# A PEER layer on one core: one-hot matrices built one token at a time, and a gate table with its rows in another order

## The chip, the cores and the metric

The kernel runs on one core of a Trainium2 chip. The metric is the device time of one execution in microseconds (us). Most executions agree within 0.3%. Five engines work side by side, each through its own instructions in order: PE (TensorE, matrix products into PSUM; PEld is its weight load), DVE (VectorE), ACT (ScalarE), POOL (GpSimd) and SP (SyncE), which here only issues transfers. Sixteen DMA engines carry out the transfers.

## The reference, cut to what matters

A decoder layer with three kinds of attention, an output projection, and a PEER feed-forward layer over 512 tokens. In the PEER part every token has 8 heads, each head picks 16 experts out of 128 x 128 by two sets of sub-keys, and the result of a token is the sum over its 128 chosen experts of gelu(u_e . h) times the gate, times v_e:

```python
expert = jnp.take_along_axis(cand_idx, pos, axis=-1)     # i1 * 128 + i2
gate = jax.nn.softmax(top_s, axis=-1)
...
a = jnp.einsum('cd,ced->ce', x_c, u[e_c])
w = jax.nn.gelu(a.astype(jnp.float32), approximate=False).astype(x_c.dtype) * g_c
return jnp.einsum('ce,ced->cd', w, v[e_c])
```

## The kernel before, in words

The attention, the projections and the query products come first. Then the 512 tokens are split in two. The 128 tokens of chunk `GC` are served by gathers: `gather_all` (lines 479 to 494) fetches one row of `u` or `v` per token and slot with an indirect DMA that POOL issues (line 475) and works on it with DVE (line 482 for `u`, line 493 for half of `v`) or with ACT and POOL (the other half). The other 384 tokens (three chunks, `DC`) are served densely: all 16384 experts are applied to all tokens, in 128 blocks of 128 experts, and a gate table says how much each expert counts for each token, mostly nothing.

Each block takes two products. `a_block` (line 521) multiplies a block of `u` with the 384 tokens, in 24 matmuls of 384 columns, and takes the gelu with ACT (line 527). `w_block` (line 628) multiplies that with the gates (line 645) and the result with a block of `v`, in 18 matmuls of 512 columns, which stay in PSUM as running sums over all 128 blocks. `u_parts` (line 514) prepares a block of `u`: SP loads it into one of three `flat` buffers (line 516), ACT writes the high part (line 86) and POOL the low part (line 87) into one of four places of `yT`.

The gate table is made in the stage that the diff touches (lines 577 to 602). For every token the 128 pairs (i1, i2) and their gates lie on the 128 partitions, as columns of `iT`. One matmul per token turns them into a 128 x 128 table: the one-hot matrix of i1, 128 slots x 128 keys, times the one-hot matrix of i2 with the gate in it. Four tokens form a group: DVE compares four columns of i1 with `iota` in one instruction of 512 elements (line 591), the same for i2 (line 592), and the gate goes in with one DVE instruction of 512 elements in every second group (line 595), and with four ACT instructions in the others (line 597). Then come four matmuls (line 600) and one ACT copy into `stage` (line 601), which holds 32 tokens as 128 keys i1 on the partitions x 128 keys i2 x 32 tokens. There are 96 groups and 12 `stage` tiles in two buffers. Line 602 writes each `stage` to a DRAM tile of its own, `gd[ci_][q]`, with the same order of axes, 16 KB in one run per partition.

In the same stretch of time 64 of the 128 `a_block`s run ahead, and their results go to DRAM (`ad`, line 607); half of the 128 `u` gathers are put beside them. From line 613 on `w_block` runs over the 128 blocks, inline `a_block`s for the other 64 blocks between them. Every four blocks it loads the gates of four blocks (`NB = 4`) from the 12 tiles: 12 transfers (line 637) in runs of 32 tokens, 128 bytes.

Tile, the layer that the kernel is written in, makes the order of instructions on each engine from the order of the source, the dependencies and a model of their times, and puts in the waits. `bank("s")` gives one of four PSUM banks.

Of the kernel before, what the change touches and what calls it, by code (L numbers as in the profile page):

```python
# [11 lines left out]
F32 = mybir.dt.float32  # L12
# [4 lines left out]
AF = mybir.ActivationFunctionType  # L17
ALU = mybir.AluOpType
# [4 lines left out]
P = 128  # L23
# [7 lines left out]
NK = 128  # L31
# [5 lines left out]
DC = [c for c in range(NT) if c != GC]  # L37
NSP = 64
GT = 32
LEAD = 2  # L40
NB = 4
# [3 lines left out]
SCB = 4  # L45
UL = "GGGG"
EM = 4
OGD = "AV"
GR = 1.0
TD = P * len(DC)  # L50
GROUPS = ((0, 1, 2), (3, 4, 5), (6, 7))
# [5 lines left out]
def layer_kernel(ctx, tc, x, xT, memT, mem, w_in, w_kv, w_out, w_q, cols, qk_gain, g_bc, subT, bias_tab,  # L57
                 uT, u, v, out):
    nc = tc.nc
    V, A, G, T, DMA = nc.vector, nc.scalar, nc.gpsimd, nc.tensor, nc.sync  # L60

    def tile_pool(**kw):
        return tc.tile_pool(reuse_waits="tile", **kw)

    top = ctx.enter_context(tc.tile_pool(name="top", bufs=1))
    dram = ctx.enter_context(tc.tile_pool(name="dram", bufs=1, space=DRAM))
    st = ctx.enter_context(tile_pool(name="st", bufs=8))
    xd = [dram.tile([P, D], F32, name=f"xd{c}") for c in range(NT)]
    gd = [[dram.tile([P, NK, GT], F32, name=f"gd{c}_{q}") for q in range(P // GT)] for c in range(len(DC))]
    ad = [dram.tile([P, TD], F32, name=f"ad{b}") for b in range(NSP)]  # L70

    ident = top.tile([P, P], F32, name="ident")
# [3 lines left out]
    iota = top.tile([P, NK], F32, name="iota")  # L76
# [8 lines left out]
    def split(hi, lo, src, e_lo=None):  # L85
        A.activation(hi, src, AF.Copy)  # L86
        return (e_lo or V).tensor_sub(lo, src, hi.bitcast(F32))  # L87
# [27 lines left out]
    def bank(tag=None):  # L115
        if tag is None:
            tag = CYC[turn[0] % len(CYC)]
            turn[0] += 1
        return pps.tile([P, S], F32, tag=tag, name=tag, bufs=BANKS[tag])

    def quarters(t):
        return t.rearrange("p (a b) -> p a b", b=P)
# [356 lines left out]
    def gather_all():  # L479
        for s_ in range(NSLOT):  # L480
            row = gather(u, s_)
            V.scalar_tensor_tensor(row, row, 1.0, hg, ALU.mult, ALU.mult, accum_out=av[:, s_:s_ + 1])  # L482
            yield
        ge = peer.tile([P, NSLOT], F32, name="ge")
        A.activation(ge, av, AF.Gelu)
        V.tensor_mul(gw, ge, gate_g)
        for s_ in range(NSLOT):
            row = gather(v, s_)
            if s_ % 2:
                A.activation(row, row, AF.Copy, scale=gw[:, s_:s_ + 1])  # L490
                G.tensor_add(ga[1], ga[1], row)  # L491
            else:
                V.scalar_tensor_tensor(ga[0], row, gw[:, s_:s_ + 1], ga[0], ALU.mult, ALU.add)  # L493
            yield
# [35 lines left out]
    with tile_pool(name="qa", bufs=1) as qa, tile_pool(name="qp", bufs=2) as qp:  # L530
# [5 lines left out]
        for n in range(4):  # L536
# [5 lines left out]
            w = [w_pieces[n, k2] for k2 in range(KD // 2)]  # L542
# [34 lines left out]
    with tile_pool(name="oh", bufs=2) as oh:  # L577
        loaded = 0
        steps = gather_all()
        for ci_, c in enumerate(DC):  # L580
            iT = oh.tile([P, 3, P], F32, tag="iT", name="iT")
            route(c, iT)
            for q in range(P // GT):
                stage = oh.tile([P, NK, GT], F32, tag="stage", name="stage")
                for t4 in range(0, GT, 4):
                    t0 = q * GT + t4
                    bc = lambda a: a[:, t0:t0 + 4, None].to_broadcast([P, 4, NK])
                    ib = iota[:, None, :].to_broadcast([P, 4, NK])
                    o1 = oh.tile([P, 4, NK], F32, tag="o1", name="o1", bufs=3)
                    o2 = oh.tile([P, 4, NK], F32, tag="o2", name="o2", bufs=3)  # L590
                    V.tensor_tensor(o1, bc(iT[:, 0, :]), ib, ALU.is_equal)  # L591
                    V.tensor_tensor(o2, bc(iT[:, 1, :]), ib, ALU.is_equal)  # L592
                    og = oh.tile([P, 4, NK], F32, tag="og", name="og", bufs=3)
                    if OGD[t4 // 4 % len(OGD)] == "V":
                        V.tensor_mul(og, o2, bc(iT[:, 2, :]))  # L595
                    for j in range(0 if OGD[t4 // 4 % len(OGD)] == "V" else 4):
                        A.activation(og[:, j, :], o2[:, j, :], AF.Copy, scale=iT[:, 2, t0 + j:t0 + j + 1])
                    gp = quarters(bank("s"))
                    for j in range(4):
                        T.matmul(gp[:, j, :], o1[:, j, :], og[:, j, :], start=True, stop=True)  # L600
                    A.activation(stage[:, :, t4:t4 + 4].rearrange("p e t -> p t e"), gp, AF.Copy)
                DMA.dma_start(gd[ci_][q], stage)
        for b in range(NSP):
            while loaded < min(b + 4, NSP):
                u_parts(loaded, loaded % 4, dict(G=G, V=V)[UL[loaded % len(UL)]])
                loaded += 1
            DMA.dma_start(ad[b], a_block(b))
            for s_ in range(int(GR * b), int(GR * (b + 1))):
                with tc.issue_after(last_lo[-1].ins):
                    next(steps)  # L610

    vs_src = v.rearrange("(a b) w -> b a w", b=NK)
    with tile_pool(name="vb", bufs=2) as vb:
        acc = [[bank("ssssoo"[2 * c + n]) for n in range(2)] for c in range(len(DC))]
        inl, spl = (list(range(r0, r1, NB)) for r0, r1 in ((NSP, NK), (0, NSP)))
        starts, a, b = [], 0, 0
        while a + b < len(inl) + len(spl):
            if a < len(inl) and (b == len(spl) or a < LEAD or (a - LEAD) * len(spl) <= b * (len(inl) - LEAD)):
                starts.append(inl[a])
                a += 1  # L620
            else:
                starts.append(spl[b])
                b += 1
        order = [b + i for b in starts for i in range(NB)]
        later = {b: a for b, a in zip([b for b in order if b >= NSP], [b for b in order if b >= NSP][1:])}
        gtiles = {}

        def w_block(n, b, ag):
            if ag is None:
                ag = vb.tile([P, TD], F32, tag="agr", name="agr", bufs=3)  # L630
                DMA.dma_start(ag, ad[b])
            g0 = b // NB * NB
            if g0 not in gtiles:
                gt = vb.tile([P, NB, len(DC), P], F32, tag="gt", name="gt")
                for ci_ in range(len(DC)):
                    for q in range(P // GT):
                        DMA.dma_start(gt[:, :, ci_, q * GT:(q + 1) * GT], gd[ci_][q][:, g0:g0 + NB, :])
                gtiles[g0] = gt
            gt = gtiles[g0]
            vr = vb.tile([P, D], F32, tag="vr", name="vr", bufs=3)  # L640
            DMA.dma_start(vr, vs_src[b])
            vs = [t.rearrange("p k t -> p (k t)")[:, (2 + n % 2) * D:(3 + n % 2) * D] for t in yT]
            split(vs[0], vs[1], vr)
            w = vb.tile([P, TD], F32, tag="w", name="w")
            V.tensor_mul(w.rearrange("p (c t) -> p c t", t=P), ag.rearrange("p (c t) -> p c t", t=P),  # L645
                         gt[:, b % NB, :, :])
            ws = [vb.tile([P, TD], F32R, tag=f"ws{i}", name=f"ws{i}") for i in range(2)]
            split(ws[0], ws[1], w)
            for ci_ in range(len(DC)):
                for k in range(2):  # L650
                    mm3(acc[ci_][k], [t[:, ci_ * P:(ci_ + 1) * P] for t in ws],
                        [t[:, k * 512:(k + 1) * 512] for t in vs], n == 0, n == NK - 1)

        pend = None
        for n, b in enumerate(order):
            if b >= NSP:
                for a in (b, later.get(b)):
                    if a is not None and a not in halves and a >= loaded:
                        u_parts(a, a % 2, G)
                        loaded = a + 1  # L660
                ag = a_block(b)
            else:
                ag = None
            if pend is not None:
                w_block(*pend)
            pend = (n, b, ag)
        w_block(*pend)
        for _ in steps:
            pass
        for c in [GC] + DC:  # L670
            xr = vb.tile([P, D], F32, tag="xr", name="xr", bufs=3)
            DMA.dma_start(xr, xd[c])
            if c == GC:
                for t in ga:
                    V.tensor_add(xr, xr, t)
            else:
                for k in range(2):
                    sl = xr[:, k * 512:(k + 1) * 512]
                    V.tensor_add(sl, sl, acc[DC.index(c)][k])
            DMA.dma_start(out[c * P:(c + 1) * P, :], xr)  # L680
# [59 lines left out]
```

## Time and profile before

| | |
|---|---|
| time, median of 3 runs | 1754.59 us (1750.6 to 1756.23) |
| span of the profiled execution, first to last instruction | 1749.3 us |
| PE busy | 1592.6 us (91%) |
| DVE busy | 1442.9 us (82%) |
| POOL busy | 968.3 us (55%) |
| ACT busy | 787.2 us (45%) |
| DMA | 390.08 MB in 317463 packets, 214944 of them under 512 B |

The profile is one execution. The page gives its span and no other time of its own; the runs, timed without a profile, lie 1.3 to 6.9 us above the span. Busy time is the union of the instructions of an engine; matmuls overlap each other, so a busy PE is not always at its peak, and two DVE instructions in a row overlap by some 0.08 us in the records, so that the cost of one is the time from its start to the next start. An engine that waits for a memory port is shown as busy.

### The profile page before, as it was taken

The numbers are of one execution on the slowest core, as the hardware profiler recorded it, in microseconds if no ns is written. First come the engines' busy times: TensorE is split into PE (matmuls) and PEld (weight loads), VectorE is DVE, ScalarE is ACT, GpSimd is POOL, SyncE is SP. The second block draws the span as 40 slices with busy tenths as digits, with TensorE's granted clock in tenths as the row PEclk, the third lists the DMA queues.
The fourth block names the chain that finished last, engine by engine and source line by source line (L and its number), as shares of the span: only waits on it lengthen the run. The fifth ranks groups of instructions, "written<-read, shape, count | busy, mean of one in ns | idle before, by whom it ended". The sixth has DMA issues, their size and how long they took to land.

```text
span 1749.3 us, 23459 instructions
## 1 busy us (share of the span) xinstructions
PE 1592.6 (91%) x8045; PEld 1397.1 (80%) x8045; DVE 1442.9 (82%) x2552; ACT 787.2 (45%) x1287; POOL 968.3 (55%) x531
## 2 busy tenths in 40 slices
PE   7999989997686878878999999999999999899997
PEld 6886667997686777778998888888888888788885
DVE  6556745899999999979956877877889978889896
ACT  6345633332332555667843333334444443444442
POOL 4220013363776675734465544456778867788774
PEclk9999999998888989889999999999999999999998
DMA  8302034132566566557699999998999999898894
GB/s 322 106 25 103 1 121 144 49 125 90 181 212 198 182 218 216 176 222 280 231 315 325 279 318 288 315 286 279 291 287 278 317 290 275 255 309 276 288 277 171
DMA packets 317463, 390.08 MB, mean 223 GB/s; under 512 B 214944, under 2 KB 240544, under 8 KB 314656
## 3 DMA queue, kind: packets, MB, share of 16 engines
q1 hardware_dynamic: 280480, 254.36, 46.0%
q0 software_dynamic: 36864, 134.23, 21.6%
q8 instruction: 63, 1.03, 0.2%
q14 instruction: 56, 0.46, 0.1%
HBM read 346.57 MB, written 41.94 MB: 222 GB/s over the span
## 4 chain that ended last, share of the span: by engine, by line
PE 49%; DVE 36%; issue 5%; DMA 5%; ACT 2%; SPq 2%; POOL 2%; DVEq 0%; ACTq 0%; POOLq 0%
PE s L96 7%; PE s L97 7%; PE s L95 6%; PE t L95 5%; PE t L97 5%; PE t L96 5%; DVE row L482 5%; DVE o L591 5%; DVE o L592 4%; PE o L96 3%; PE o L97 3%; PE o L95 3%; DVE eq L440 2%; PE o L330 2%; DVE og L595 2%
## 5 line engine op out<-in xcount | busy, mean ns | idle before, releaser
L87 POOL TENSOR_TENSOR yT<-flat,yT 128x1024 fp32r<-128x1024 f32 x128 | 346.6, 2709 | 216.4 <-ACT yT L86 208.7
L95 PE MATMUL t<-hT,yT 128*128 128x384 f32 x1024 | 351.4, 343 | 26.1 <-ACT ag L527 26.1
L97 PE MATMUL t<-hT,yT 128*128 128x384 f32 x1024 | 351.4, 343 | 2.4 <-POOL yT L87 2.4
L96 PE MATMUL t<-hT,yT 128*128 128x384 f32 x1024 | 350.3, 342 | 0.0
L87 DVE TENSOR_TENSOR yT<-vr,yT 128x1024 fp32r<-128x1024 f32 x128 | 209.5, 1637 | 54.7 <-ACT yT L86 51.5
L475 POOL DMA_INDIRECT row<-u,exp_g x128 | 161.7, 1263 | 124.0 <-DVE row L482 88.3
L95 PEld LDWEIGHTS t<-hT,yT 128*128 128x128 f32 x1024 | 197.0, 192 | 32.5 <-ACT ag L527 27.3
L96 PE MATMUL s<-yT,ws 128*128 128x512 f32 x512 | 206.7, 405 | 11.1 <-DVE yT L87 10.8
L482 DVE SCALAR_TENSOR_TENSOR row<-row,hg 128x1024 f32<-128x1024 f32 x128 | 189.2, 1482 | 24.0 <-DMA row<-u,exp_g 24.0
L97 PE MATMUL s<-yT,ws 128*128 128x512 f32 x512 | 201.4, 402 | 4.2 <-DVE ws L87 4.2
L475 POOL DMA_INDIRECT row<-v,exp_g x128 | 156.1, 1219 | 84.9 <-DVE ga L493 49.6
L86 ACT ACTIVATE ws<-w 128x384 fp32r<-128x384 f32 x128 | 67.1, 524 | 299.4 <-DVE w L645 118.7
L97 PEld LDWEIGHTS t<-hT,yT 128*128 128x128 f32 x1024 | 196.8, 192 | 5.7 <-POOL yT L87 3.0
L96 PEld LDWEIGHTS t<-hT,yT 128*128 128x128 f32 x1024 | 196.8, 192 | 4.5
L86 ACT ACTIVATE yT<-flat 128x1024 fp32r<-128x1024 f32 x128 | 135.4, 1058 | 144.2 <-issue 53.6
L491 POOL TENSOR_TENSOR ga<-ga,row 128x1024 f32<-128x1024 f32 x64 | 164.1, 2564 | 26.1 <-ACT row L490 25.4
L95 PE MATMUL s<-yT,ws 128*128 128x512 f32 x512 | 165.1, 399 | 7.8 <-ACT ws L86 7.8
L86 ACT ACTIVATE yT<-vr 128x1024 fp32r<-128x1024 f32 x128 | 134.2, 1048 | 57.4 <-DMA vr<-v 44.0
L600 PE MATMUL s<-og,o 128*128 128x128 f32 x768 | 109.7, 296 | 54.8 <-DVE og L595 38.4
L600 PEld LDWEIGHTS s<-og,o 128*128 128x128 f32 x768 | 103.1, 208 | 63.4 <-issue 39.6
L87 DVE TENSOR_TENSOR ws<-w,ws 128x384 fp32r<-128x384 f32 x128 | 119.8, 937 | 41.0 <-ACT ws L86 36.2
L493 DVE SCALAR_TENSOR_TENSOR ga<-row,gw,ga 128x1024 f32<-128x1024 f32 x64 | 143.2, 2238 | 6.6 <-DMA row<-v,exp_g 6.4
(268 smaller groups left out, 3249.2 us busy)
## 6 DMA issues: line engine op xcount, KB each, us to landing
flat<-uT SPq DMA_DIRECT2D x128, 512.0 KB
vr<-v SPq DMA_DIRECT2D x128, 512.0 KB
gd<-stage SPq DMA_DIRECT2D x12, 2048.0 KB
gt<-gd SPq DMA_DIRECT2D x384, 64.0 KB
ad<-ag SPq DMA_DIRECT2D x64, 192.0 KB
agr<-ad SPq DMA_DIRECT2D x64, 192.0 KB
wraw<-w_in SPq DMA_DIRECT2D x8, 1024.0 KB
flat<-w_q SPq DMA_DIRECT2D x16, 512.0 KB
```

Of the source, the lines that this page charges most:

```text
L86: A.activation(hi, src, AF.Copy)
L87: return (e_lo or V).tensor_sub(lo, src, hi.bitcast(F32))
L95: T.matmul(o, ah, bh, start=start, stop=False)
L96: T.matmul(o, ah, bl, start=False, stop=False)
L97: T.matmul(o, al, bh, start=False, stop=stop)
L475: G.indirect_dma_start(out=row, out_offset=None, in_=table, in_offset=bass.IndirectOffsetOnAxis(ap=exp_g[:, s_:s_ + 1], axis=0))
L482: V.scalar_tensor_tensor(row, row, 1.0, hg, ALU.mult, ALU.mult, accum_out=av[:, s_:s_ + 1])
L491: G.tensor_add(ga[1], ga[1], row)
L493: V.scalar_tensor_tensor(ga[0], row, gw[:, s_:s_ + 1], ga[0], ALU.mult, ALU.add)
L591: V.tensor_tensor(o1, bc(iT[:, 0, :]), ib, ALU.is_equal)
L592: V.tensor_tensor(o2, bc(iT[:, 1, :]), ib, ALU.is_equal)
L600: T.matmul(gp[:, j, :], o1[:, j, :], og[:, j, :], start=True, stop=True)
```

## The change

The comparison with i1 and the one with i2 become one DVE instruction each per token, of 128 elements, with the token's column of `iT` as a scalar operand (one value per partition). The second instruction also multiplies with the gate, a second scalar operand. The tile `og`, its DVE instruction and its four ACT instructions go. The gate table becomes one DRAM tile with the axes block (i2), expert (i1), token; line 602 writes it in runs of 32 tokens, and every four blocks it is read by one transfer in runs of 384 tokens. Line 645 then multiplies tiles that are contiguous.

```diff
-OGD = "AV"
...
-    gd = [[dram.tile([P, NK, GT], F32, name=f"gd{c}_{q}") for q in range(P // GT)] for c in range(len(DC))]
+    gd = dram.tile([NK, P, TD], F32, name="gd")
...
-                    bc = lambda a: a[:, t0:t0 + 4, None].to_broadcast([P, 4, NK])
-                    ib = iota[:, None, :].to_broadcast([P, 4, NK])
                     o1 = oh.tile([P, 4, NK], F32, tag="o1", name="o1", bufs=3)
                     o2 = oh.tile([P, 4, NK], F32, tag="o2", name="o2", bufs=3)
-                    V.tensor_tensor(o1, bc(iT[:, 0, :]), ib, ALU.is_equal)
-                    V.tensor_tensor(o2, bc(iT[:, 1, :]), ib, ALU.is_equal)
-                    og = oh.tile([P, 4, NK], F32, tag="og", name="og", bufs=3)
-                    if OGD[t4 // 4 % len(OGD)] == "V":
-                        V.tensor_mul(og, o2, bc(iT[:, 2, :]))
-                    for j in range(0 if OGD[t4 // 4 % len(OGD)] == "V" else 4):
-                        A.activation(og[:, j, :], o2[:, j, :], AF.Copy, scale=iT[:, 2, t0 + j:t0 + j + 1])
+                    for j in range(4):
+                        i1, i2, gate = (iT[:, i, t0 + j:t0 + j + 1] for i in range(3))
+                        V.tensor_scalar(o1[:, j, :], iota, i1, None, ALU.is_equal)
+                        V.tensor_scalar(o2[:, j, :], iota, i2, gate, ALU.is_equal, ALU.mult)
                     gp = quarters(bank("s"))
                     for j in range(4):
-                        T.matmul(gp[:, j, :], o1[:, j, :], og[:, j, :], start=True, stop=True)
+                        T.matmul(gp[:, j, :], o1[:, j, :], o2[:, j, :], start=True, stop=True)
...
-                DMA.dma_start(gd[ci_][q], stage)
+                DMA.dma_start(gd[:, :, ci_ * P + q * GT:ci_ * P + (q + 1) * GT].rearrange("b p t -> p b t"), stage)
...
-                gt = vb.tile([P, NB, len(DC), P], F32, tag="gt", name="gt")
-                for ci_ in range(len(DC)):
-                    for q in range(P // GT):
-                        DMA.dma_start(gt[:, :, ci_, q * GT:(q + 1) * GT], gd[ci_][q][:, g0:g0 + NB, :])
+                gt = vb.tile([P, NB, TD], F32, tag="gt", name="gt")
+                DMA.dma_start(gt, gd[g0:g0 + NB].rearrange("b p t -> p b t"))
...
-            V.tensor_mul(w.rearrange("p (c t) -> p c t", t=P), ag.rearrange("p (c t) -> p c t", t=P),
-                         gt[:, b % NB, :, :])
+            V.tensor_mul(w, ag, gt[:, b % NB])
```

## Rows read from the trace of the kernel before

**Rows 1.** By stretch: busy us of PE, PEld, DVE, ACT, POOL; clock, DMA share, GB/s.

```profile
560.00:880.00 320.00, 265.24 (x1661) 256.54 (x1660) 311.09 (x375) 204.66 (x367) 181.59 (x82) 0.93 0.60 217
900.00:1700.00 800.00, 781.62 (x3686) 674.21 (x3685) 660.58 (x561) 334.39 (x431) 537.18 (x306) 1.00 0.93 293
```

**Rows 2.** The chain that ended last, 560 to 880 us, shares by line.

```profile
by line: DVE o L591 24.8%; DVE o L592 23.5%; DVE row L482 15.0%; DVE og L595 10.9%; DMA row<-u,exp_g 6.6%; DVE eq L440 4.4%; DVE ex L443 3.9%; issue 3.4%; DVE eq L442 3.1%; PE s L600 1.5%; DVE pe L447 0.7%; PE t L97 0.5%; PE t L96 0.4%; PE 
```

**Rows 3.** Groups by line, 560 to 880: busy us, mean ns | idle before, releasers.

```profile
L591 DVE TENSOR_TENSOR o<-iT,iota 128x512 f32<-128x512 f32 x96 | 96.7, 1022 | 0.0
L592 DVE TENSOR_TENSOR o<-iT,iota 128x512 f32<-128x512 f32 x96 | 89.5, 955 | 0.0
L595 DVE TENSOR_TENSOR og<-o,iT 128x512 f32<-128x512 f32 x48 | 41.6, 868 | 0.0
L87 POOL TENSOR_TENSOR yT<-flat,yT 128x1024 fp32r<-128x1024 f32 x37 | 113.9, 3080 | 127.0 <-ACT yT L86 126.8
L475 POOL DMA_INDIRECT row<-u,exp_g x37 | 48.7, 1317 | 5.6 <-issue 2.6 <-PE s L600 0.2
```

**Rows 4.** Timeline of DVE, then of POOL beside it: start us, duration us.

```profile
562.82 2.88 DVE L592 TENSOR_TENSOR o<-iT,iota 128x512 f32<-128x512 f32 x1
565.62 0.68 DVE L591 TENSOR_TENSOR o<-iT,iota 128x512 f32<-128x512 f32 x1
566.22 0.68 DVE L592 TENSOR_TENSOR o<-iT,iota 128x512 f32<-128x512 f32 x1
...
562.23 2.92 POOL L87 TENSOR_TENSOR yT<-flat,yT 128x1024 fp32r<-128x1024 f32 x1 [3.65 <-ACT yT L86]
565.30 1.24 POOL L475 DMA_INDIRECT row<-u,exp_g  x1
```

**Rows 5.** Timeline of DVE: scalar operand per partition, then a constant.

```profile
145.40 0.28 DVE L313 TENSOR_SCALAR p<-p,den 128x128 f32<-128x128 f32 x1
145.59 0.15 DVE L312 RECIPROCAL den<-den 128x1 f32<-128x1 f32 x1
...
553.72 0.21 DVE L464 TENSOR_SCALAR e<-ei 128x128 int32<-128x128 int32 x1
553.86 0.21 DVE L465 TENSOR_SCALAR e<-ei 128x128 int32<-128x128 int32 x1
```

**Rows 6.** Groups by form: the same operation from PSUM, and a blocked CAST.

```profile
L217 DVE TENSOR_SCALAR vt<-s,rx 128x128 f32<-128x128 f32 x2 | 0.7, 343 | 0.0
L421 DVE CAST tf<-ti 128x128 f32<-128x128 uint32 x3 | 3.4, 1121 | 0.0
```

**Rows 7.** DMA queues, 560 to 880, then 900 to 1700: packets, MB, share.

```profile
q1 hardware_dynamic: 12240, 49.75, 43.1%
...
q1 hardware_dynamic: 236289, 136.84, 58.5%
q0 software_dynamic: 26640, 97.01, 33.9%
gt<-gd SPq DMA_DIRECT2D x377, 64.0 KB
```

**Rows 8.** Timeline of SP's transfers: start us, time to issue them, how many.

```profile
880.58 0.32 SPq L602 DMA_DIRECT2D gd<-stage  x1
882.97 0.32 SPq L607 DMA_DIRECT2D ad<-ag  x1
...
887.56 11.18 SPq L637 DMA_DIRECT2D gt<-gd  x6
...
908.55 6.17 SPq L607 DMA_DIRECT2D ad<-ag  x1
914.77 8.73 SPq L637 DMA_DIRECT2D gt<-gd  x10
...
934.41 12.87 SPq L637 DMA_DIRECT2D gt<-gd  x10
```

**Rows 9.** The chain that ended last, 738 to 780 us: start us, us.

```profile
740.17 10.87 DMA row<-u,exp_g
```

More of the change, by code (lines that the diff above doesn't have):

```diff
@@ L644, in w_block @@
             w = vb.tile([P, TD], F32, tag="w", name="w")
-            V.tensor_mul(w.rearrange("p (c t) -> p c t", t=P), ag.rearrange("p (c t) -> p c t", t=P),
-                         gt[:, b % NB, :, :])
+            V.tensor_mul(w, ag, gt[:, b % NB, :])
             ws = [vb.tile([P, TD], F32R, tag=f"ws{i}", name=f"ws{i}") for i in range(2)]
```

## The prediction

> **What bounds the kernel now.** I read the busy times by stretch first. In the stage that makes the gate table, 560 to 880 us, DVE is busy for 311.1 of 320 us and PE for 265.2; from 900 to 1700 us PE is busy for 781.6 of 800 [rows 1]. So the stage is DVE's and what follows is PE's, with 55 us of idle PE in the one and 18.4 us in the other. The chain that ended last says the same: in the stage the two comparisons and the DVE half of the gate product hold 59% of it, the gather product of line 482 another 15% [rows 2]. A microsecond that DVE loses or wins there should move the end; one in the later stretch counts only as far as it touches PE's 18.4 us.
>
> The groups of the stage show how DVE's time is made up [rows 3]. The 240 instructions of lines 591, 592 and 595 are busy for 227.8 us. In the timeline an undisturbed one starts 0.60 us after the one before and is shown with 0.68 us; another takes 2.88 us, and beside that one POOL works on line 87 from 562.23 to 565.15 [rows 4]. 240 x 0.68 = 163 us, so some 65 us of the 227.8 are time behind POOL.
>
> **The change part by part.** First DVE's own work. Now: 240 x 0.60 = 144 us. After: 384 tokens x 2 = 768 instructions of 128 elements. The nearest row is the softmax scaling, 128x128 with one scalar operand per partition, source and result in SBUF: it starts at 145.40 and the next starts at 145.59, 0.19 to 0.20 us (12 such) [rows 5]. With a constant in its place the step is 0.14 us (553.72 to 553.86), so I put the operand at 0.06 us. Line 591's successor: 384 x 0.195 = 75 us. Line 592's has two such operands, and no row shows that; I take another 0.06 us, 384 x 0.255 = 98 us, since the first cost that much. Together 173 us, +29 us. Bounds: 0.14 us for all, if the operands cost nothing here, gives 104 us, -40 us; the same operation with its source in PSUM lasts 0.343 us [rows 6], some 0.265 from start to start, which gives 204 us, +60 us.
>
> Four small instructions per comparison thus cost DVE about what the one large one did: 8 x 0.195 = 1.56 us a group against 2.5 x 0.60 = 1.50 us, even with the gate free of charge. The 192 ACT instructions that go I cost at nothing: ACT is busy for 204.7 of the 320 us [rows 1], and is no line of the stage's chain [rows 2].
>
> Second, the wait behind POOL. The 37 low parts of line 87 keep their number and their length. A small CAST of 128x128 also waits: its three come to 1.12 us on average [rows 6], though such a one lasts 0.21 us undisturbed. I leave the 65 us as they are. If smaller steps let POOL in less often or more often, that is worth -65 us at most, and upward the rest of POOL's 113.9 us, +49 us.
>
> Third, POOL's indirect DMAs. The comparison at 565.62 lasted its 0.68 us although POOL was issuing a gather from 565.30 to 566.54 [rows 4], so they do not hold a comparison of two tensors. No row shows a scalar-operand instruction beside a gather alone. Bounds: nothing, or all 48.7 us of the 37 gathers [rows 3]; I take 10 us, nearer to the row that shows no wait. The Trainium skill, in "SBUF — State Buffer", section "Who interferes with whom", says that a `tensor_scalar` whose operands allow it runs in a mode that takes the port pair shared with GpSimd whole, and that the generation of descriptors needs that pair's write side, while a two-tensor instruction takes the read side only. The undisturbed comparison agrees with the second half; by the first half the whole of it, 49 us, would come into the sum in place of 10.
>
> Fourth, the writes of the gate table. A `stage` of 2 MB now leaves in 128 runs of 16 KB, after the change in 128 x 128 = 16384 runs of 128 bytes. The table of before is read in such runs, and from 900 to 1700 us one can price them [rows 7]. The gathers' queue q0 moved 97.01 MB in 33.9% of 16 x 800 us, 22.4 bytes per ns. Queue q1 moved 136.84 MB in 58.5%, 7488 us of engine time; 377 x 64 KB = 24.7 MB of it, in 193,000 runs, are the gate loads, and the other 112.1 MB at 22.4 bytes per ns make 5005 us. That leaves 2483 us, an estimated 12.9 ns a run. One write is then 16384 x 12.9 / 16 = 13.2 us on all 16 engines, against 5.9 us for 2.1 MB at 22.4 bytes per ns. In the stage the DMA engines have 0.60 of 320 us in use [rows 1], 192 us; +88 us makes 280 us, still below 320.
>
> But SP issues in order, and what it issues behind a write waits: the loads of `u` (line 516) and the writes of line 607. Now a write occupies SP for 0.32 us. In the busy later stretch ten gate loads of 512 runs each took SP 8.73 and 12.87 us [rows 8], which is 28 to 41 us for 16384 runs. So a write holds SP and its queue for 13 to 41 us. Writes come every 320 / 12 = 26.7 us. In that time 3.1 blocks of `u` (37 in the stage [rows 3]) need 3.1 x 1.46 us of the engines and their results 3.1 x 0.55 us, so a hold of up to 20.5 us fits. The cover for one hold is the four places of `yT`: at 320 / 37 = 8.6 us a block they last 35 us. I take a hold of 18 us, nearer to the lower end because the stage's DMA share is 0.60 and the later stretch's 0.93, and 10 us for PE starved now and then; bounds: 0, and 12 x (41 - 20.5) = 246 us. In return a gather's landing may become shorter than the 10.87 us that it took at 740.17 [rows 9], since 4 KB rows would then stand beside runs of 128 bytes on the engines; landings like this hold 6.6% of the stage's chain [rows 2], 21 us, and with the longer writes beside them I cost it at nothing.
>
> Fifth, the reads and the passage to them. 384 loads become 32, in runs of 1536 bytes: 25.2 MB at 22.4 bytes per ns, 70 us of the 16 engines in place of 158, and some 350 issues less on SP. PE can only win its 18.4 us of idle time there; I take 10, bounds 0 and 18. Where the first load waits for the last write (issue at 880.58, first load at 887.56 [rows 8]) the longer write costs some 11 us, and the 24 issues that held SP there until 923 go; I set these against each other.
>
> Last, a longer stage lets PE do what it now has left at its end: five blocks of `a_block`, whose results go out from 882.97 to 908.55 [rows 8], 26 us. Since their order is laid down beforehand I count 5 us of that; bounds 0 and 26.
>
> Sum: +29 + 10 + 10 - 10 - 5 = +34 us. On the profiled execution's span of 1749.3 us that is 1783 us; the median of the runs lies 5.3 us above that span, so 1788 us.
>
> **The rivals.** (a) The gate writes become the bound of the stage. At 28 us a hold, 12 x (28 - 20.5) = 90 us are missing in the queue, the loads of `u` come late and PE starves; with 10 us back from the reads, +80 us, 1835 us. It decides from a hold of about 24 us, where its loss passes DVE's 39 us. For it: the 28 to 41 us of SP's rows. Against it: the 13.2 us at the packets' own price. The Trainium skill, "DMA: Bandwidth & Descriptors", section "Specifications", has a rule of this kind: transfers under 512 bytes run below line rate, because the engine reads, changes and writes back. The trace agrees for reads (9.9 against 22.4 bytes per ns) and has no write so small. Were a written run twice a read one, a hold would be 26 us and the rival's case would be met.
>
> (b) The relief of the later stretch wins: not slower. The second operand is free (+6 us of DVE in place of 29), gathers do not hold the new instructions, the writes fit, and PE's idle time after 900 us goes whole, -18 us, with 9 of the gathers' 21 us on the chain: -21 us, 1733 us. It decides where the stage grows by less than the reads give back. For it: 88 us less DMA time at a DMA share of 0.93. Against it: PE is busy for 98% there already.
>
> (c) The stage grows by some 20 us and PE fills that with its five blocks: no change, 1755 us. Against it: PE's order is fixed before the run.
>
> **How the numbers follow.** Forecast (1765 to 1815 us): 0.46. Rival (a): 0.22. Rival (b): 0.20. Rival (c): 0.12. The measurement tells 0.3%, about 5 us, from no change. Faster: (b), 0.20. Within: (c), 0.12. Slower: the forecast and (a), 0.68. The range leaves out the lower half of (b) and the far end of (a): 1742 to 1855 us.
>
> **What would show it.** In the profile after, the comparisons of i1 start 0.19 to 0.20 us apart and those of i2 0.25 to 0.26; DVE stays full from 560 us to a stage end that is some 30 us later; single instructions still last 2 to 3 us beside line 87. The 12 writes hold SP for about 18 us each; a step from one to the next SP issue near 28 us speaks for (a), with PE idle and DVE not full. Steps of 0.19 us for both, and a stage that ends at 880 us, would make the forecast wrong.

## The result, and the profile after

The changed kernel takes 1803.4 us (1800.93 to 1803.61, four runs) against 1755.4 us (1750.6 to 1756.6, four runs). The measured ratio is 1.0297, with a 95% interval of 1.0259 to 1.0335, or +52 us, 45 to 59; the two medians by themselves give 1.0273, +48 us, which lies in that interval. The profiled executions differ by 52.5 us. Below, too, "+n us" is the ratio less one, times the time of before, about 1750 us, with its interval behind it. The forecast was +34 us.

The span of the profiled execution is 1801.8 us. Busy times by stretch, in the columns of [rows 1]: the stage, which now ends with the last write's issue at 920.12 us in place of 880.58, and 800 us behind it.

```profile
560.00:920.00 360.00, 299.70 (x1758) 285.92 (x1757) 356.37 (x907) 157.85 (x181) 153.63 (x85) 0.91 0.94 198
940.00:1740.00 800.00, 761.36 (x3509) 651.55 (x3510) 671.20 (x553) 328.82 (x420) 554.45 (x313) 0.97 0.84 296
```

DVE is still full in the stage, and the stage is 39.5 us longer; the forecast's terms for it were +29 and +10. What was not in the forecast is the second row: PE, which was to gain there, now idles for 39 of 800 us. In [rows 1] it idled for 18.4.

The groups of the stage, 560 to 920 us, answer to [rows 3]:

```profile
L591 DVE TENSOR_SCALAR o<-iota,iT 128x128 f32<-128x128 f32 x384 | 165.1, 430 | 0.0
L590 DVE TENSOR_SCALAR o<-iota,iT 128x128 f32<-128x128 f32 x384 | 163.8, 427 | 3.6 <-PE s L594 3.5
L481 DVE SCALAR_TENSOR_TENSOR row<-row,hg 128x1024 f32<-128x1024 f32 x41 | 52.6, 1300 | 0.0
...
L86 POOL TENSOR_TENSOR yT<-flat,yT 128x1024 fp32r<-128x1024 f32 x38 | 93.7, 2465 | 112.3 <-ACT yT L85 109.8 <-PE t L95 2.3
L474 POOL DMA_INDIRECT row<-u,exp_g x39 | 45.1, 1155 | 91.0 <-DVE row L481 39.5 <-DVE o L590 38.6 <-PE t L95 5.8
```

And the timeline of DVE, then of POOL beside it (start us, duration us), answers to [rows 4]:

```profile
693.79 0.28 DVE L590 TENSOR_SCALAR o<-iota,iT 128x128 f32<-128x128 f32 x1
693.99 0.34 DVE L591 TENSOR_SCALAR o<-iota,iT 128x128 f32<-128x128 f32 x1
694.25 2.97 DVE L590 TENSOR_SCALAR o<-iota,iT 128x128 f32<-128x128 f32 x1
697.14 0.33 DVE L591 TENSOR_SCALAR o<-iota,iT 128x128 f32<-128x128 f32 x1
697.40 0.27 DVE L590 TENSOR_SCALAR o<-iota,iT 128x128 f32<-128x128 f32 x1
697.59 0.33 DVE L591 TENSOR_SCALAR o<-iota,iT 128x128 f32<-128x128 f32 x1
697.85 0.27 DVE L590 TENSOR_SCALAR o<-iota,iT 128x128 f32<-128x128 f32 x1
...
694.72 2.41 POOL L86 TENSOR_TENSOR yT<-flat,yT 128x1024 fp32r<-128x1024 f32 x1
697.28 1.02 POOL L474 DMA_INDIRECT row<-u,exp_g  x1 [0.16 <-PE t L96]
```

The steps are 0.20 us for i1 and 0.26 us for i2 with the gate (medians over all of them: 0.196 and 0.256). One comparison waits out POOL's low part, 2.97 us; the four beside the gather of 697.28 run undisturbed.

### The profile page after: what moved, and what is told of

The parts are those of the page before. It is cut to its first block, busy times and chain, and to the rows that moved or that the text cites. A ratio compares the mean times of both kernels' runs of the same rounds, so it can differ in the third digit from the quotient of the medians.

```text
span 1801.8 us, 23320 instructions
## 1 busy us (share of the span) xinstructions
PE 1624.9 (90%) x8045; PEld 1419.1 (79%) x8045; DVE 1491.2 (83%) x3080; ACT 736.5 (41%) x1095; POOL 940.8 (52%) x531
## 4 chain that ended last, share of the span: by engine, by line
PE 43%; DVE 38%; POOL 6%; DMA 5%; issue 5%; ACT 2%; DVEq 0%; SPq 0%; POOLq 0%; ACTq 0%
DVE o L590 7%; DVE o L591 6%; PE s L96 6%; PE s L95 6%; PE s L94 6%; DVE row L481 4%; DMA row<-v,exp_g 4%; PE t L94 4%; PE t L96 4%; PE t L95 4%; PE o L95 3%; PE o L96 3%; PE o L94 3%; DVE eq L439 2%; DVE yT L86 2%
## 5 line engine op out<-in xcount | busy, mean ns | idle before, releaser
L86 POOL TENSOR_TENSOR yT<-flat,yT 128x1024 fp32r<-128x1024 f32 x128 | 321.2, 2509 | 245.3 <-ACT yT L85 241.6
L94 PE MATMUL t<-hT,yT 128*128 128x384 f32 x1024 | 362.6, 354 | 36.0 <-ACT ag L526 24.3
L96 PE MATMUL t<-hT,yT 128*128 128x384 f32 x1024 | 362.3, 354 | 5.2 <-POOL yT L86 5.2
L95 PE MATMUL t<-hT,yT 128*128 128x384 f32 x1024 | 361.1, 353 | 0.0
L94 PEld LDWEIGHTS t<-hT,yT 128*128 128x128 f32 x1024 | 200.8, 196 | 42.3 <-ACT ag L526 25.6
L96 PE MATMUL s<-yT,ws 128*128 128x512 f32 x512 | 206.8, 409 | 19.0 <-DVE ws L86 18.8
L95 PE MATMUL s<-yT,ws 128*128 128x512 f32 x512 | 207.2, 405 | 9.6 <-DVE yT L86 9.6
L96 PEld LDWEIGHTS t<-hT,yT 128*128 128x128 f32 x1024 | 200.2, 196 | 9.6 <-POOL yT L86 6.7
L95 PEld LDWEIGHTS t<-hT,yT 128*128 128x128 f32 x1024 | 200.6, 196 | 4.3
L594 PE MATMUL s<-o,o 128*128 128x128 f32 x768 | 153.3, 305 | 56.0 <-DVE o L591 52.9
L474 POOL DMA_INDIRECT row<-v,exp_g x128 | 164.3, 1284 | 64.8 <-DVE ga L492 30.2
L86 DVE TENSOR_TENSOR ws<-w,ws 128x384 fp32r<-128x384 f32 x128 | 133.5, 1043 | 71.5 <-ACT ws L85 68.4
L594 PEld LDWEIGHTS s<-o,o 128*128 128x128 f32 x768 | 137.4, 211 | 69.0 <-DVE o L591 39.0
L481 DVE SCALAR_TENSOR_TENSOR row<-row,hg 128x1024 f32<-128x1024 f32 x128 | 179.4, 1414 | 12.6 <-DMA row<-u,exp_g 12.6
L94 PE MATMUL s<-yT,ws 128*128 128x512 f32 x512 | 169.9, 403 | 2.7 <-ACT ws L85 2.7
L590 DVE TENSOR_SCALAR o<-iota,iT 128x128 f32<-128x128 f32 x384 | 163.8, 427 | 3.6 <-PE s L594 3.5
L591 DVE TENSOR_SCALAR o<-iota,iT 128x128 f32<-128x128 f32 x384 | 165.1, 430 | 0.0
```

The source lines that it names most:

```text
L94: T.matmul(o, ah, bh, start=start, stop=False)
L95: T.matmul(o, ah, bl, start=False, stop=False)
L96: T.matmul(o, al, bh, start=False, stop=stop)
L474: G.indirect_dma_start(out=row, out_offset=None, in_=table, in_offset=bass.IndirectOffsetOnAxis(ap=exp_g[:, s_:s_ + 1], axis=0))
L590: V.tensor_scalar(o1[:, j, :], iota, i1, None, ALU.is_equal)
L591: V.tensor_scalar(o2[:, j, :], iota, i2, gate, ALU.is_equal, ALU.mult)
```

## Which half costs what

The change has two halves, which can be made one at a time. The first two runs do that.

**The one-hot instructions alone**, on the table of before: the diff's lines around `V.tensor_scalar`, and nothing else.

> The one-hot half of the change alone; the gate table keeps its 12 DRAM tiles and the loads in runs of 128 bytes. Theory A (DVE's own time and its longer wait behind POOL make the loss): +40 to +55 us against before, some 1800 us, and the stage ends near 915 us. Theory B (the 128-byte writes hold SP's queue and make the loss): +0 to +15 us, and the stage ends near 890 us. In either case the steps between the instructions are 0.195 and 0.255 us.

Measured: 1.0148 [1.0107, 1.0189], +26 us [19, 33]. That lies between the two expectations, so neither range was met. The last write's issue is at 946.51 us, later than either theory had it. DVE is busy for 320.0 of the 320 us from 560 to 880, as theory A has it, but this longer stage also holds more work: all the `a_block`s that run ahead, and 57 products of the gathers where before's stage has 40.

**The table alone**, with the one-hot instructions of before: the diff's lines on `gd`, on `gt` and on the gate product.

> The layout half alone; the comparisons and the gate product are those of before. Theory A: -10 to +8 us against before, since the writes fit into the queue and the later stretch has little idle PE time to win. Theory B: +35 to +50 us, with SP held 11 us and more behind each write and PE idle for it.

Measured: 1.0184 [1.0138, 1.0230], +32 us [24, 40]. The size is nearer to theory B, whose range begins at 35, but its reason, PE idle behind the writes, is not what the run shows. The half that was to give 10 us back costs as much as the one-hot half, and the two add up to the whole within the intervals: 26 + 32 = 58, against 45 to 59. The stretches of this run show where:

```profile
560.00:880.00 320.00, 268.97 (x1676) 259.68 (x1675) 308.91 (x370) 202.61 (x368) 172.61 (x78) 0.93 1.02 209
1200.00:1600.00 400.00, 366.76 (x1667) 311.27 (x1666) 356.39 (x222) 177.70 (x218) 332.49 (x185) 0.96 0.83 287
```

In the stage nothing is lost: PE and DVE are busy as in [rows 1], although the DMA share went from 0.60 to 1.02. The loss lies behind it. In the same 400 us before has this:

```profile
1200.00:1600.00 400.00, 387.61 (x1810) 332.33 (x1809) 343.59 (x233) 181.93 (x228) 299.87 (x166) 0.99 0.90 286
```

PE does 8% fewer matmuls with the new table, while the DMA engines do less.

**The gate left out**, in the whole change, so that both instructions have one scalar operand:

```diff
-                        V.tensor_scalar(o2[:, j, :], iota, i2, gate, ALU.is_equal, ALU.mult)
+                        V.tensor_scalar(o2[:, j, :], iota, i2, None, ALU.is_equal)
```

> The changed kernel without the gate in the second comparison (left out: the product with the gate), so that each of the 768 instructions has one scalar operand. If the second operand costs 0.06 us and DVE sets the stage's end: 384 x 0.06 = 23 us less than the changed kernel, some 1780 us. If DVE is not the bound any more since the writes hold the queue: within 5 us of the changed kernel, some 1803 us.

Measured: 1.0193 [1.0158, 1.0228], +34 us [28, 40], 18 us below the change; the price of the second operand, 384 x 0.06 = 23 us, lies within what the two intervals allow, and the steps of both instructions are 0.196 us here. The run does not price the operand by itself, though. The order of the instructions on the engines differs from the change's, the last write's issue is 40 us earlier (879.71 us), and ACT's wait for rows of `v`, the subject of the next section, is 62.8 us between 1200 and 1600 us in place of 46.9.

**512-byte runs** in place of 128, one load per group as in the change, with the one-hot instructions of before:

```diff
+    gd = dram.tile([NK // NB, P, TD // GT, NB * GT], F32, name="gd")
...
+                DMA.dma_start(gd[:, :, ci_ * (P // GT) + q, :].rearrange("g p x -> p g x"),
+                              stage.rearrange("p (g n) t -> p g (n t)", n=NB))
...
+                DMA.dma_start(gt.rearrange("p c n t -> p c (n t)"), gd[b // NB])
```

> The comparisons of before with a third layout: for each four blocks, key, group of 32 tokens, then 4 blocks x 32 tokens in one run; written in runs of 512 bytes (4096 a write), read by one transfer in 32 in runs of 6 KB. If the 128-byte loads of before cost PE's idle time after 900 us: -10 to -18 us against before, 1737 to 1745 us. If PE's order alone sets that stretch: within 5 us of before.

Measured: 1.0165 [1.0126, 1.0205], +29 us [22, 36]: neither. The DMA share of the stage was back at 0.67, and the loss stayed. So 128-byte writes are not what it needs.

## Where the table's half loses it

In the table alone, ACT waits for rows of `v`. This is its wait for them between 1200 and 1600 us (us in total, times, longest us):

```profile
ACT row L490 <- DMA row<-v,exp_g: 50.5, 22, 4.7
```

and the same of before:

```profile
ACT row L490 <- DMA row<-v,exp_g: 9.3, 5, 3.6
```

ACT works in its own order. While it waits for a row, the split of `w` (`ws`) and that of `v` (`yT`) stand behind it, and PE waits for them. These are all of PE's waits in the same 400 us, in the table alone:

```profile
PE s L96 <- DVE yT L87: 15.5, 5, 6.2
PE s L97 <- DVE ws L87: 12.6, 7, 4.2
PE s L95 <- ACT ws L86: 5.2, 4, 2.6
```

and before:

```profile
PE s L96 <- DVE yT L87: 6.8, 5, 2.0
PE s L95 <- ACT ws L86: 3.7, 2, 3.2
PE s L97 <- DVE ws L87: 1.7, 1, 1.7
```

They differ by the 21 us that PE is busy less. Most of them name DVE, which makes the low parts of both splits behind ACT and which itself waits for rows of `v`, 18.2 us in the table alone and not at all before; below, ACT's waits stand for both. POOL issues 105 gathers in these 400 us where before has 92 (the rows of line 475), and they end earlier: the last is issued at 1634.56 us, before at 1720.77. My first theory was therefore that the gathers are too dense. Its tests were two, both with the table alone.

**Read in 12 loads**, as before:

```diff
-                DMA.dma_start(gt, gd[g0:g0 + NB].rearrange("b p t -> p b t"))
+                for t0 in range(0, TD, GT):
+                    DMA.dma_start(gt[:, :, t0:t0 + GT], gd[g0:g0 + NB, :, t0:t0 + GT].rearrange("b p t -> p b t"))
```

> Before's one-hot instructions with the changed table in DRAM (block, expert, token; written in 128-byte runs as in the change), but read as before in 12 loads of 64 KB per group of four blocks instead of one of 768 KB. Theory A: the layout half's +35 us comes from the single load: with 12 issues per group the order of the gathers of v is spread to the end of the later stretch as before, with one it is denser and ends some 90 us early; so here -5 to +10 us against before (1745 to 1760), PE's idle time after the stage back at some 25 us, last gather after 1700 us. Theory B: it comes from the table's layout and its 128-byte writes: +25 to +40 us as in the layout half alone.

Measured: 1.0040 [1.0018, 1.0061], +7 us [3, 11]. Most of the loss is gone, with the same writes. ACT's wait is 2.3 us.

**Gathers tied to the blocks**, with one load:

```diff
             if pend is not None:
                 w_block(*pend)
+            for _ in range(3 if b >= NSP else 0):
+                with tc.issue_after(last_lo[-1].ins):
+                    next(steps, None)
```

> The layout half alone (one load of 768 KB per group), with the remaining gathers tied to the blocks: after each of the 64 later a_blocks, three gather steps are issued behind POOL's low part of that block, so none can come earlier. Theory A (the gathers' order is what costs): most of the +35 us goes, +0 to +12 us against before (1750 to 1762). Theory C (the one large load itself holds the queue and so the gathers and the loads of v): +25 us or more stays, with ACT and DVE waiting on the rows of v as long as in the layout half alone (56 and 19 us).

Measured: 1.0282 [1.0242, 1.0323], +49 us [42, 57]. Only 83 gathers fall into the 400 us, and ACT's wait grew:

```profile
ACT row L490 <- DMA row<-v,exp_g: 74.3, 27, 7.7
```

So theory A fell in the form that the gathers are too dense: fewer of them in the same time do not help.

**The same on the grouped table:**

> Before's one-hot instructions, the table grouped so that it is written in 512-byte runs and read in one load per group, and the gathers tied to the blocks as in the run beside it. Theory A: +0 us or a few us below before (1742 to 1755), since the stage ends 6 us earlier in the grouped table and the rest is as before. Theory C: +20 us or more stays.

Measured: 1.0244 [1.0190, 1.0298], +43 us [33, 52]. The same.

Theory C named the size of the loss in both runs, but its reason, that the large load slows the gathers, does not hold either: between 1200 and 1600 us a row lands 6.7 us after its issue (median) with ties and one load, and 6.4 us with 12 loads. What differs is how soon after the issue ACT gets to the row. I paired the 64 gathers of `v` that ACT works on with its instructions, and took the time from POOL's issue to the end of ACT's instruction ahead. The median is 9.0 us before, 9.3 with 12 loads, 6.2 in the table alone, 5.3 with the ties and 6.2 in the change. Turns that come within 6.5 us of the issue, about when a row lands, are 20, 15, 34, 48 and 38 of the 64. The order on the engines puts the work closer behind its gather, and the gather is not faster.

That order is laid down before the run, from a model of times. The next runs ask what in the loads moves it: their number, or the length of their runs.

**Four loads of 128-byte runs**, with the writes of the change:

```diff
-                DMA.dma_start(gt, gd[g0:g0 + NB].rearrange("b p t -> p b t"))
+                for n_ in range(NB):
+                    DMA.dma_start(gt[:, :, n_, :], gd[g0 + n_].rearrange("p (c t) -> p c t", t=GT))
```

> The layout half alone, with the gates of a group read in 4 loads of 192 KB, one per block, whose runs are 128 bytes (the tile in SBUF is laid out so that 32 tokens lie together); before has 12 loads of 128-byte runs, the layout half one load of 1536-byte runs. Theory A (the order of the instructions is made from a model of the transfers' times; with long runs the model thinks the transfers short, and puts the work on a row of v earlier behind its gather than the row lands): with 128-byte runs the order has later turns again, whatever the number of loads; +0 to +10 us against before, ACT's waits for rows of v near before's 22 us. Theory B (the number of loads is what counts): at 4 loads most of the +35 us stays, +20 to +35.

Measured: 0.9988 [0.9967, 1.0010], -2 us [-6, 2].

**Twelve loads of 512-byte runs**, on the grouped table:

```diff
-                DMA.dma_start(gt.rearrange("p c n t -> p c (n t)"), gd[b // NB])
+                for c0 in range(0, TD // GT, 1):
+                    DMA.dma_start(gt[:, c0:c0 + 1].rearrange("p c n t -> p c (n t)"), gd[b // NB][:, c0:c0 + 1])
```

> The grouped table (written in 512-byte runs), read in 12 loads of 64 KB per group as in before, but in runs of 512 bytes. Theory A: the order is as dense as with one load, so the loss stays, +20 to +32 us against before, with ACT waiting 50 us or more for rows of v. Theory B (number of loads): back to before, -5 to +8 us.

Measured: 1.0126 [1.0084, 1.0168], +22 us [15, 29].

**Twelve loads of 128-byte runs**, on the same grouped table; only the order of the axes of `gt` in SBUF differs from the run before:

```diff
+                for c0 in range(TD // GT):
+                    DMA.dma_start(gt[:, :, c0 * GT:(c0 + 1) * GT], gd[b // NB][:, c0, :].rearrange("p (n t) -> p n t", t=GT))
```

> The grouped table, written in 512-byte runs, and read in 12 loads of 128-byte runs per group, with before's one-hot instructions. Theory A: the order of the gathers as before; 0 to -7 us against before (the stage of the grouped table ended 6 us earlier), the gate product contiguous. Theory B (layout in DRAM costs): +10 us or more.

Measured: 0.9995 [0.9970, 1.0020], -1 us [-5, 4].

Theory A's side came about in all three (the first lies 2 us below its range, within the interval). The last two kernels differ only in the order of the axes of `gt`, and so in the length of the runs in which the loads arrive and in how line 645 reads the tile (850 and 862 ns a product, no difference to speak of). The shorter runs win by 1.3%.

The traces show what else differs. With 128-byte runs every engine's order of instructions, by operation and tile, is before's from first to last: 1287 of ACT, 531 of POOL, 2552 of DVE, 8045 matmuls and 874 transfers of SP. With 512-byte runs it is another order: ACT comes to its last row of `v` behind the 104th split of `w`, in place of the 126th. There PE needs 454 us from its 5500th to its 7400th matmul, in place of 413, and 143 us from there to the end, in place of 158, as the gathers are done by then. So 41 us are lost where gathers and `w_block`s run side by side, and 15 won back. Over all runs, with or without the one-hot half, those 1900 matmuls take 413 to 421 us with loads in 128-byte runs and 442 to 460 with longer ones.

One gather in POOL's timeline and what ACT does until it works on the row (start us, us), first with 512-byte runs:

```profile
1412.93 1.34 POOL L475 DMA_INDIRECT row<-v,exp_g  x1 [0.30 <-issue]
...
1415.51 1.04 ACT L86 ACTIVATE yT<-vr 128x1024 fp32r<-128x1024 f32 x1
1420.72 1.15 ACT L490 ACTIVATE row<-row,gw 128x1024 f32<-128x1024 f32 x1 [4.17 <-DMA row<-v,exp_g]
1421.78 0.51 ACT L86 ACTIVATE ws<-w 128x384 fp32r<-128x384 f32 x1
```

and with 128-byte runs:

```profile
1438.93 1.03 POOL L475 DMA_INDIRECT row<-v,exp_g  x1 [2.55 <-DVE ga L493]
...
1447.43 1.04 ACT L86 ACTIVATE yT<-vr 128x1024 fp32r<-128x1024 f32 x1
1448.38 1.14 ACT L490 ACTIVATE row<-row,gw 128x1024 f32<-128x1024 f32 x1
```

In the first, ACT's turn comes 3.6 us after the issue (1416.55 - 1412.93) and it stands for 4.17 us, with `ws` behind it. In the second it comes 9.5 us after, and nothing waits. The runs in one table, without those with tied gathers and without the gate; us against before, PE's busy time and ACT's wait between 1200 and 1600 us:

| one-hots, writes, loads per group | against before | PE busy | ACT waits for rows of `v` |
|---|---|---|---|
| before: 16 KB; 12 of 128 B | | 387.6 | 9.3 |
| table alone: 128 B; 1 of 1536 B | +32 | 366.8 | 50.5 |
| grouped: 512 B; 1 of 6 KB | +29 | 363.5 | 74.9 |
| table: 128 B; 12 of 128 B | +7 | 392.7 | 2.3 |
| table: 128 B; 4 of 128 B | -2 | 391.1 | 6.7 |
| grouped: 512 B; 12 of 512 B | +22 | 367.1 | 59.1 |
| grouped: 512 B; 12 of 128 B | -1 | 392.5 | 7.6 |
| one-hots: 16 KB; 12 of 128 B | +26 | 394.0 | 5.4 |
| change: 128 B; 1 of 1536 B | +52 | 373.8 | 46.9 |
| change, 128 B; 12 of 128 B | +39 | 391.3 | 3.9 |
| change, grouped 512 B; 12 of 128 B | +34 | 394.0 | 4.7 |

Wherever the loads arrive in runs of 128 bytes, ACT waits for less than 10 us and PE is busy for 387 us or more; wherever they are longer, ACT waits for 46 us or more and PE is busy for 374 us or less. Neither the number of loads, nor the writes, nor the order of the table decides. That the model takes long runs for quicker, and so expects rows of `v` sooner, is what fits, but it is not shown: no run gives the model's own times. Nor does a run have long runs in before's order. That the order costs the time, and not the transfers, is argued from the equal landings and the earlier turns.

Two runs tried this on the whole change.

**The change, read in 12 loads** (the diff of the first such run):

> The whole change, but the gates read in 12 loads of 128-byte runs per group as before. Theory A: only the one-hot half's cost is left, +22 to +32 us against before, 20 to 30 us below the change as it is. If the two halves' losses have one cause, or the loss is in the 128-byte writes: +40 us or more.

Measured: 1.0224 [1.0177, 1.0271], +39 us [31, 47], some 13 us below the change. That lies between the two expectations; the interval reaches into both. **The change on the grouped table**, read in 12 loads of 128-byte runs:

> The change's one-hot instructions with the grouped table: written in 512-byte runs, read in 12 loads of 128-byte runs per group. It differs from the change read in 12 loads (+42 us) in the writes alone. If the 128-byte writes, or the order that is made with them, hold 10 us or so of that, as the prediction's fourth step put it: +26 to +34 us against before, like the one-hot half alone on before's table (+30). If they cost nothing and the +42 is what the one-hot half costs with any table of this kind: +38 to +46.

Measured: 1.0197 [1.0164, 1.0230], +34 us [29, 40]. The two intervals overlap, and that of the one-hot half on before's table, 19 to 33, reaches into both. The run on the grouped table has the very order of that half, on every engine, so the two measure one order with two tables. So the long runs hold some 13 of the change's 52 us (2 to 23 by the two intervals) and the one-hot half 26 to 34. The 13 are a net: from PE's 5500th to its 7400th matmul the change takes 452 us and the change read in 12 loads 418, from there to the end 145 and 165, as the latter's last gather is issued at 1767.03 us and the former's at 1653.29.

What the 128-byte writes hold, 5 us by the last two runs with -5 to 15 allowed, is not settled. One thing that stands behind them can be seen in the change, where the stage ends. SP's transfers (start us, time to issue):

```profile
920.12 0.37 SPq L596 DMA_DIRECT2D gd<-stage  x1
923.94 17.25 SPq L515 DMA_DIRECT2D flat<-uT  x1
941.25 0.42 SPq L601 DMA_DIRECT2D ad<-ag  x1
```

the chain that ended last, from there on (start us, us):

```profile
923.94 20.78 DMA flat<-uT
944.79 1.11 issue
945.94 2.36 POOL yT L86
```

and the stretches around PE's restart, in the columns of [rows 1]:

```profile
940.00:946.00 6.00, 0.09 (x1) 0.09 (x1) 1.77 (x4) 1.20 (x2) 0.06 (x1) 0.64 0.89 267
946.00:952.00 6.00, 4.58 (x14) 4.07 (x15) 2.24 (x1) 1.29 (x2) 5.67 (x4) 0.51 1.04 414
952.00:960.00 8.00, 8.00 (x48) 8.00 (x47) 5.19 (x6) 4.65 (x7) 5.33 (x4) 1.00 1.04 411
```

SP stood for 17 us with a load of `u` behind the last write. PE's longest wait is there, 9.5 us, and after it the granted clock was 0.51, the lower of its two levels (1.2 GHz), until 952 us: 14 matmuls in 6 us, then 48 in 8. In the run of the change with 12 loads the same wait was 9.1 us. On the grouped table it is absent, but there PE stands once for 27.2 us at the first `w_block`, since all early blocks are done by then. So the wait is not where the two runs part: PE begins its 4700th matmul at 1039.0 us in the run with 12 loads and at 1049.9 on the grouped table. The latter wins later, at the end above all (148 us from the 7400th matmul, in place of 165).

## The prediction, step by step

**DVE's own work, +29 us: right.** The steps are 0.196 and 0.256 us at the median, 384 x 0.452 = 174 us against 144, +30. The second operand did cost what the first one costs.

**The wait behind POOL, unchanged: wrong, +14 us in the sum.** Undisturbed ones are shown with 0.28 and 0.34 us, 384 x 0.62 = 238 us of the 328.9, so 91 us stand behind POOL, not 65. Others wait less, 12 us in all: the gather product fell from 1481 to 1300 ns each, 7 us together, and six products of the router from 10.4 to 5.8 us. And the low parts did not keep their length: 2465 ns each, before 3080.

**The gathers, +10 us: wrong, 0.** The row of 697.28 shows it, and of the 130 comparisons that ran beside a gather and no other POOL instruction the mean delay was 0.01 us. The rule of the Trainium skill ("SBUF — State Buffer", section "Who interferes with whom"), by which 49 us would have come in, is not borne out on DVE's side; no run shows in which mode these instructions ran. Nor are the gathers longer, 1155 ns against 1317 [rows 3]; but POOL's idle time ahead of them grew from 5.6 to 91.0 us, put down to DVE's gather product and to the comparisons. Whether a held port has a part in that no run here tells. POOL is not what the stage waits for.

Together the three steps were to make the stage 29 + 10 us longer, and it is 39.5 us longer. That the sum fits is luck: it is 30 of own work, 26 more behind POOL on the new instructions, 12 less on the others, 0 beside the gathers, and 5 us less of idle DVE (3.6 us in the 360, before 8.9 in the 320).

**The writes, +10 us: not settled.** The price of a run was too low. From [rows 7] it came to 12.9 ns; in the table alone the stage's DMA share rose by 0.42 of 16 x 320 us, 2150 us, over 196608 runs and in place of some 1130 us for 16 KB runs: an estimated 16.7 ns a run, 17 us a write. The hold, 18 us as taken, was 17.25 us at the last write and 5.4 to 14.3 at the eleven others, and 19.3 at most in the table alone. All are below the 20.5 us that fit, so (a) did not come about: in the table alone PE's busy time in the stage is 269.0 us, before 265.2. The rule that transfers under 512 bytes run below line rate (the Trainium skill, "DMA: Bandwidth & Descriptors", section "Specifications") agrees with the shares: 0.67 with 512-byte runs, 1.02 with 128. The stage itself did not feel it; behind its end a few us show. In the four runs with 128-byte writes and before's one-hots PE begins its 4700th matmul 451 to 453 us after it restarts ahead of the stage (behind a wait of 13 us), before and in the four runs with 512-byte writes 443 to 448 us after. Whether the transfers do that, or the order that is laid out with them and differs within the stage already, no run separates; the whole time of one of the four is that of before (-2 us [-6, 2]).

**The reads, -10 us: this is the step that failed.** It went by DMA time: less of it, so PE could only win its 18.4 us, with bounds of 0 and -18. The DMA time did fall (the share from 0.90 to 0.83 in the table alone between 1200 and 1600 us), and PE lost 21 us in those 400; in place of -10 the table alone measured +32 us, and +7 with 128-byte runs in the loads. The bounds left out that the loads are part of what the order of all engines is made from. With loads in longer runs the order brought ACT to the rows of `v` some 3 us sooner after their issue, before many of them had landed: 34 of 64 turns within 6.5 us of the issue, before 20.

**The passage to the reads, 0:** the 11 us on the one side came in the change, as 9.5 us of PE's wait and a few us at the lower clock. Whether the issues that went gave anything back no run shows.

**PE's filling of the longer stage, -5 us:** not measured by itself. In the run of the one-hot half alone all `a_block`s that run ahead end within the stage, which is then 386 us long.

So the direction was right for the reason given, DVE's work in the stage, +26 us with the one-hot half alone. The size was near by luck: the stage's terms were off one by one and fit in the sum, and a loss in place of a gain in the reads was small enough for the range.

## What to carry to other kernels

Where a planner lays the order of instructions down from modelled times, a transfer that gets cheaper is an edit of every engine's order: after such a change look first at the waits for other transfers, and at the time from their issue to the turn of their consumer. A loss with less DMA time and more idle PE is the sign. And two kernels that differ in the length of the runs alone can differ in the order of every engine: compare the two sequences of instructions before a difference in time is put down to the transfer.

## What was not expected of the hardware

A DMA share of 1.02 over the stage, against 0.60, did not make the stage longer (the share adds up the times of all packets, so that it can pass 1): in the table alone the last write's issue is at 881.02 us, before at 880.58, and the kernel with these writes and four loads of 128-byte runs ran at 0.9988 [0.9967, 1.0010]. And 12 loads in 128-byte runs in place of 512 made no difference to the landing of the gathers beside them (6.5 against 6.4 us, median; of the latter half are recorded), though they hold the engines longer, 0.91 against 0.84 of the 16 between 1200 and 1600 us.
